# Key centring on GpSimd, fewer screening tiles on ScalarE, and six score banks, in a threshold attention kernel

## Chip, cores and metric

The kernel runs on one core of one Trainium2 chip. The metric is the device time of one execution in microseconds (us), the median of several runs. Engines are PE (TensorE, with PEld for its weight loads), DVE (VectorE), ACT (ScalarE), POOL (GpSimd) and SP (SyncE, which only issues transfers here). To evict a tile is to copy it out of PSUM, where this kernel's matmuls put their results, into SBUF, where they find their operands. The span runs from the first to the last instruction of the profiled run. The granted clock is the share of TensorE's full clock that the profile shows it was given; half-clock time is the time for which its records stand at 0.5.

## The reference

Attention over 8 x 12 heads, 512 positions, 64 dimensions, in which only weights above a threshold are kept and then normalised again:

```python
scores = einsum('bhqd,bhkd->bhqk', Q, K) / sqrt(64)
weights = softmax(scores)
weights = where(weights > 0.1, weights, 0)
weights = weights / (sum(weights) + 1e-10)
out = einsum('bhqk,bhkd->bhqd', weights, V)
```

## The kernel before

With random inputs very few rows have any weight above 0.1. The kernel screens all rows cheaply in fp16 and computes only the suspects exactly. Heads go in pairs (hp, 48 of them), and two pairs make a group q (24 groups). For each pair PE transposes keys and queries, ACT evicts the keys and sums them, the queries are evicted by ACT or DVE, and the keys are centred: 512 k - sum(k), in fp16. Eight score tiles of 128x512 per pair follow. Each is screened either by ACT (sum of exponentials) or by DVE (maximum); the table `ACT_TILES` says which. Then comes a chain per group on small tiles: flags, ranks, indices, gather of the suspect queries, exact scores, gather of a value row, scatter to the output.

```python
def do_kev(hp):                                   # ACT
    ...
    keep(nc.scalar.activation(kt[:], sc[:], ACTF.Copy, accum_out=ksum[:]))

def do_kcentre(hp):                               # DVE: the centring
    keep(nc.vector.tensor_scalar(T["qk", hp][:, 1, :], T["kt", hp][:], CS, T.pop(("ksum", hp))[:, 0:1],
                                 op0=ALU.mult, op1=ALU.subtract))

def do_sizes(hp):                                 # DVE: "sq", absolute values, reads the centred keys
    ...
    keep(nc.vector.tensor_scalar(sq..., T["qk", hp]..., 0x7FFF, None, op0=ALU.bitwise_and))

def do_screen(g, h2):
    ...
    if (h2, qi) in ACT_TILES[tiles_of(hp // 2)]:
        keep(nc.scalar.activation(junk[:], sc[:], ACTF.Exp, scale=BETA * scale / CS, accum_out=at))
    else:
        keep(nc.vector.tensor_reduce(at, sc[:], axis=AX.X, op=ALU.max))
```

The order of instructions on every engine is fixed beforehand by a small planner in the kernel. Each step is entered with an engine, the time for which it occupies it and the time to its result, both written in by hand. The engines then run their lists strictly in that order:

```python
add(("kc", hp), ("DVE", 0.46, 0.55), [("kev", hp), ("qev", hp)], g0 - 4, lambda hp=hp: do_kcentre(hp))
add(("sq", hp), ("DVE", 0.40, 0.52), [("kc", hp)], g0 + 3, lambda hp=hp: do_sizes(hp))
...
add(("qk", g), ("PE", 0.33, 0.45), [("kc", hp)], g - 2, ...)
```

The softmax here doesn't subtract the row's maximum and nothing guards it: scores larger than these inputs give would overflow.

Of the kernel before, what the change touches and what calls it, by code (L numbers as in the profile page):

```python
# [102 lines left out]
def kernel(  # L103
# [28 lines left out]
    nc = tc.nc  # L132
# [3 lines left out]
    SO = S // P  # L136
# [5 lines left out]
    scale = 1.0 / float(D) ** 0.5  # L142
# [8 lines left out]
    keep = tc.keep_in_program_order  # L151
# [8 lines left out]
    CUT = (S - 1.0) / S * math.log(max(odds, 1e-30)) - MARGIN  # L160
    CUT_SUM = 0.995 * math.exp(max(-80.0, min(80.0, BETA * CUT)))

    CS = float(S)


    ACT_TILES = ({(0, 0), (0, 1), (0, 2), (0, 3), (1, 2)},
                 {(0, 0), (0, 1), (0, 2), (0, 3), (1, 1), (1, 3)})

    def tiles_of(q):
        return 0 if q < NQ - 2 else 1  # L170
# [72 lines left out]


    cuts = consts.tile([P, 2, 2, C2], f32)
    nc.gpsimd.memset(cuts[:], CUT_SUM)
    for which in range(2):
        for h2 in range(2):
            for qi in range(SO):
                if (h2, qi) not in ACT_TILES[which]:  # L250
                    nc.gpsimd.memset(cuts[:, which, :, h2 * SO + qi], CUT * CS / scale)


    TOP_UNIT = 2.0 ** (8 * 0.0861 + 7)
# [21 lines left out]
    vpool = ctx.enter_context(tc.tile_pool(name="v", bufs=2))  # L276
    tpool = ctx.enter_context(tc.tile_pool(name="t", bufs=5))
    ktpool = ctx.enter_context(tc.tile_pool(name="kt", bufs=14))
    SC, SM = 5, 3
    spsum = ctx.enter_context(tc.tile_pool(name="spsum", bufs=SC, space=bass.MemoryType.PSUM))  # L280
    mpsum = ctx.enter_context(tc.tile_pool(name="mpsum", bufs=SM, space=bass.MemoryType.PSUM))
    junkp = ctx.enter_context(tc.tile_pool(name="junk", bufs=2))
# [6 lines left out]
    T = {}  # L289
# [20 lines left out]
    def zero_fill(q):  # L310
        fills[q] = nc.sync.dma_start(out=Oz[q], in_=zero[:])
        for s in scatters.values():
            tc.declare_no_dep(fills[q].ins, s.ins, reason="other rows of the output")
# [8 lines left out]
    def do_ktr(hp):  # L322
        T["ktr", hp] = transpose_pair(T.pop(("k", hp)))

    def do_qtr(hp):
        T["qtr", hp] = transpose_pair(T.pop(("q", hp)))

    def do_kev(hp):
        sc = T.pop(("ktr", hp))
        kt = ktpool.tile([P, SO * P], f32)  # L330
        ksum = small.tile([P, 1], f32)
        keep(nc.scalar.activation(kt[:], sc[:], ACTF.Copy, accum_out=ksum[:]))  # L332
        T["kt", hp], T["ksum", hp] = kt, ksum
# [4 lines left out]
    def do_qev(hp, eng):  # L338
        qk = tpool.tile([P, 2, SO * P], SCREEN)
        copy(eng, qk[:, 0, :], T.pop(("qtr", hp))[:])  # L340
        T["qk", hp] = qk

    def do_kcentre(hp):
        keep(nc.vector.tensor_scalar(T["qk", hp][:, 1, :], T["kt", hp][:], CS, T.pop(("ksum", hp))[:, 0:1],  # L344
                                     op0=ALU.mult, op1=ALU.subtract))


# [16 lines left out]
    def do_screen(g, h2):  # L364
        hp, qi = divmod(g, SO)
        if ("stat", hp // 2) not in T:
            stat = small.tile([P, 2, C2], f32)
            T["stat", hp // 2] = stat
        c = h2 * SO + qi
        at = T["stat", hp // 2][:, hp % 2, c:c + 1]  # L370
        sc = T.pop(("sc", g, h2))
        if (h2, qi) in ACT_TILES[tiles_of(hp // 2)]:
            junk = junkp.tile([P, SO * P], bf16)
            keep(nc.scalar.activation(junk[:], sc[:], ACTF.Exp, scale=BETA * scale / CS, accum_out=at))  # L374
        else:
            keep(nc.vector.tensor_reduce(at, sc[:], axis=AX.X, op=ALU.max))  # L376
# [169 lines left out]
    def add(name, ways, deps, prio, fn, takes=(), gives=()):  # L546
        sched.add(name, [ways] if isinstance(ways, tuple) else ways, deps, prio, fn, takes, gives)

    for hp in range(NP):
        q, n = divmod(hp, 2)  # L550
        g0 = hp * SO
        for kind, tr, fn, d in (("k", "ktr", load_k, 0.0), ("q", "qtr", load_q, 0.1)):
            add((kind, hp), ("DMA", 1.2, 3.3), [] if hp < 5 else [(tr, hp - 5)], g0 - 20 + d,
                lambda fn=fn, hp=hp: fn(hp))
        if n == 0:
            add(("z", q), ("DMA", 1.8, 4.0), [], g0 - 7.5, lambda q=q: zero_fill(q))
        ahead = [] if hp < 4 else [("qk", g0 - 3 * SO - 1), ("sq", hp - 4)]
        add(("ktr", hp), ("PE", 0.53, 0.65), [("k", hp)] + ahead, g0 - 7, lambda hp=hp: do_ktr(hp),
            takes=[("sc", ("ktr", hp))])
        add(("qtr", hp), ("PE", 0.53, 0.65), [("q", hp)] + ahead, g0 - 6, lambda hp=hp: do_qtr(hp),  # L560
            takes=[("sc", ("qtr", hp))])
        add(("kev", hp), ("ACT", 0.60, 0.85), [("ktr", hp)], g0 - 6, lambda hp=hp: do_kev(hp),
            gives=[("sc", ("ktr", hp))])
        add(("qev", hp), [("ACT", 0.47, 0.65), ("DVE", 0.60, 0.72)], [("qtr", hp)], g0 - 5,
            lambda eng, hp=hp: do_qev(hp, eng), gives=[("sc", ("qtr", hp))])
        add(("kc", hp), ("DVE", 0.46, 0.55), [("kev", hp), ("qev", hp)], g0 - 4, lambda hp=hp: do_kcentre(hp))
        add(("sq", hp), ("DVE", 0.40, 0.52), [("kc", hp)], g0 + 3, lambda hp=hp: do_sizes(hp))
        for qi in range(SO):
            g = g0 + qi
            add(("qk", g), ("PE", 0.33, 0.45), [("kc", hp)], g - 2, lambda g=g: do_qk(g),  # L570
                takes=[("sc", ("qk", g, 0)), ("sc", ("qk", g, 1))])
            for h2 in range(2):
                way = ("ACT", 0.61, 0.85) if (h2, qi) in ACT_TILES[tiles_of(q)] else ("DVE", 0.60, 0.75)
                add(("s", g, h2), way, [("qk", g)], g, lambda g=g, h2=h2: do_screen(g, h2),
                    gives=[("sc", ("qk", g, h2))])
        if n == 0:
            continue
        x = g0 + SO - 1 + LAG
        every = [("s", g, h2) for g in range(8 * q, 8 * q + 8) for h2 in range(2)]
        first = {"flags": every, "rank": [("sq", hp - 1), ("sq", hp)]}  # L580

        def stage(name, ways, deps, fn, takes=(), gives=()):
            choice = isinstance(ways, list)
            add((name, q), ways, [(d, q) for d in deps] + first.get(name, []), x,
                (lambda eng, q=q: fn(q, eng)) if choice else (lambda q=q: fn(q)), takes=takes, gives=gives)

        stage("flags", ("DVE", 0.10, 0.25), [], do_flags)
        stage("rank", ("PE", 0.75, 0.9), ["flags"], do_rank, takes=[("sm", ("rk", q))])
        stage("key", ("DVE", 0.15, 0.3), ["rank"], do_key, gives=[("sm", ("rk", q))])
        stage("oh", ("DVE", 0.62, 0.75), ["key"], do_onehot)  # L590
        stage("idx", ("PE", 0.5, 0.65), ["oh"], do_idx, takes=[("sm", ("ix", q))])
        stage("idxev", ("DVE", 0.12, 0.25), ["idx"], do_idxev)
        stage("rows", ("DVE", 0.1, 0.25), ["idx", "idxev"], do_rows, gives=[("sm", ("ix", q))])
        late = FAR if q < NQ - 3 else NEAR
        stage("gather", ("POOL", 1.2, late), ["idxev"], do_gather)
        stage("split", ("DVE", 0.2, 0.35), ["gather", "rows"], do_split)
        stage("xtr", ("PE", 0.15, 0.35), ["split"], do_xtr, takes=[("sm", ("xp", q))])
        stage("xev", [("ACT", 0.23, 0.33), ("DVE", 0.22, 0.32)], ["xtr"], do_xev, gives=[("sm", ("xp", q))])
        stage("xqk", ("PE", 1.0, 1.15), ["xev"], do_xqk, takes=[("sc", ("xs", q))])
        stage("xexp", ("ACT", 0.61, 0.85), ["xqk"], do_xexp, gives=[("sc", ("xs", q))])  # L600
        stage("xlimit", ("DVE", 0.12, 0.25), ["xexp"], do_xlimit)
        stage("xpick", ("DVE", 0.75, 0.95), ["xlimit"], do_xpick)
        stage("xone", ("DVE", 0.22, 0.35), ["xpick"], do_xone)
        stage("xto", ("DVE", 0.1, 0.25), ["xone"], do_xto)
        stage("vgather", ("POOL", 1.2, late), ["xone"], do_vgather)
        stage("scatter", ("POOL", 1.1, 3.0), ["xto", "vgather", "z"], do_scatter)
        if q == NC1 - 1:
            add(("check", 0), ("DVE", 1.8, 1.9), [("key", q)], x + 9, lambda: do_check(0))
        if q == NQ - 1:
            add(("check", 1), ("DVE", 0.35, 0.5), [("key", q)], x + 30, lambda: do_check(1))  # L610
            add(("check", 2), ("DVE", 0.3, 0.5), [("xpick", q)], x + 31, lambda: do_check(2))
# [25 lines left out]
    with tc.If(many > 0):  # L637
        with tc.For_i(0, NP, 1) as hp:
# [8 lines left out]
            kt = ktpool.tile([P, SO * P], f32)  # L647
# [69 lines left out]
```

## Time and profile before

| | before |
|---|---|
| median of 3 runs | 256.13 us (254.54 to 257.73) |
| span of the profiled run | 252.3 us |
| DVE, ACT, PE, POOL busy | 207.7, 202.1, 208.3, 82.2 us |
| mean granted TensorE clock | 0.911 |

In a row of a group, the figures after the bar are total busy us, mean ns of one, then the idle time of that engine just before such instructions and what ended it. The prediction quotes the lines that matter. It does not show the waits for scores as rows of the view of waits, which is ordered by total (columns: engine and waiting instruction, what it waited for, us in all, times, longest us):

```profile
DVE stat L376 <- PE sc L360: 9.6, 13, 2.2
ACT junk L374 <- PE sc L360: 8.1, 17, 1.1
```

### The profile page before, as it was taken

How to read it: one execution, taken by the hardware profiler on the slowest of the kernel's cores; microseconds unless marked ns; L12 is line 12 of the kernel's file. 1: busy time of each engine (PE TensorE's matmuls, PEld its weight loads, DVE VectorE, ACT ScalarE, POOL GpSimd, SP SyncE). 2: the span in 40 equal slices, each digit the busy share in tenths (PEclk: the TensorE clock that was granted, in tenths of full speed). 3: DMA queues.
4: the chain of work that ended last, by engine and by line, in shares of the span. 5: the costliest groups of instructions: out<-in, count | busy, mean ns of one | idle time of the engine just before them, and what ended most of it. 6: DMA issues, size and time to landing. Idle time of an engine off the chain costs nothing. (4 is left out here: it accounts for less than half of the span.)

```text
span 252.3 us, 5581 instructions
## 1 busy us (share of the span) xinstructions
PE 208.3 (83%) x1683; PEld 103.3 (41%) x1683; DVE 207.7 (82%) x578; ACT 202.1 (80%) x661; POOL 82.2 (33%) x121
## 2 busy tenths in 40 slices
PE   7678896898998998999898898988889998999200
PEld 3335453454443454445344544544445533324000
DVE  1788998998859999998999899999899889667220
ACT  2799998997879999987999889989989799883100
POOL 8100113334232333243163333415333213543430
PEclk9999999998979999997999799999999689559965
DMA  5899998999975898988889445564460000000000
GB/s 116 193 246 240 245 256 232 245 238 240 251 208 126 269 269 251 282 224 232 244 284 239 110 104 124 115 150 108 107 142 11 6 0 4 8 2 4 3 5 0
DMA packets 107167, 38.67 MB, mean 153 GB/s; under 512 B 103657, under 2 KB 104028, under 8 KB 107136
## 3 DMA queue, kind: packets, MB, share of 16 engines
q1 hardware_dynamic: 104832, 37.76, 56.9%
q0 software_dynamic: 2304, 0.53, 1.5%
q8 instruction: 14, 0.23, 0.4%
q14 instruction: 17, 0.14, 0.2%
HBM read 26.74 MB, written 13.37 MB: 159 GB/s over the span
## 5 line engine op out<-in xcount | busy, mean ns | idle before, releaser
L374 ACT ACTIVATE junk<-sc 128x512 bf16<-128x512 f32 x244 | 143.9, 612 | 8.6 <-PE sc L360 8.1
L376 DVE TENSOR_REDUCE stat<-sc 128x1 f32<-128x512 f32 x140 | 94.5, 684 | 10.3 <-PE sc L360 9.6
L360 PE MATMUL sc<-qk 64*128 64x512 f16 x384 | 83.3, 401 | 10.6 <-ACT junk L374 7.3
L374 ACT ACTIVATION_READ_ACCUMULATOR junk<-sc 128x1 f32 x244 | 54.2, 222 | 0.0
L508 POOL DMA_INDIRECT out_dram<-vsel,oidx x24 | 25.4, 1059 | 63.3 <-DVE rows L431 9.4
L501 POOL DMA_INDIRECT vsel<-in_V_dram,vidx x24 | 25.1, 1046 | 55.7 <-DVE oidx L497 22.1
L360 PEld LDWEIGHTS <-qk 64*128 64x128 f16 x384 | 18.2, 94 | 53.1 <-issue 49.8
L435 POOL DMA_INDIRECT qsel<-in_Q_dram,idx x24 | 25.4, 1060 | 41.8 <-DVE idx L425 30.6
L318 PE MATMUL sc<-identity_f,k_sb 128*128 128x128 f32 x192 | 33.3, 300 | 6.4 <-ACT junk L374 3.3
L332 ACT ACTIVATE kt<-sc 128x512 f32<-128x512 f32 x48 | 29.5, 615 | 6.8 <-PE sc L318 6.5
L318 PE MATMUL sc<-identity_f,q_sb 128*128 128x128 f32 x192 | 32.3, 294 | 2.0 <-ACT kt L332 1.1
L465 PE MATMUL sc<-kt,xq 128*64 128x512 f32 x96 | 30.4, 714 | 3.2 <-ACT junk L374 1.7
L318 PEld LDWEIGHTS sc<-identity_f,k_sb 128*128 128x128 f32 x192 | 21.7, 148 | 25.0 <-ACT junk L374 9.7
L472 ACT ACTIVATE e<-sc 128x512 f32<-128x512 f32 x24 | 14.4, 601 | 17.6 <-PE sc L465 17.4
L344 DVE TENSOR_SCALAR qk<-kt,ksum 128x512 f16<-128x512 f32 x48 | 24.2, 503 | 4.5 <-ACT kt L332 4.5
L318 PEld LDWEIGHTS sc<-identity_f,q_sb 128*128 128x128 f32 x192 | 23.1, 150 | 11.2 <-ACT kt L332 4.1
L336 DVE CAST qk<-sc 128x512 f16<-128x512 f32 x29 | 19.8, 686 | 7.5 <-PE sc L318 7.4
L350 DVE TENSOR_SCALAR sq<-qk 128x1024 uint16<-128x1024 uint16 x48 | 19.8, 421 | 0.3
L419 PEld LDWEIGHTS <-oh 128*128 128x128 f16 x192 | 14.4, 165 | 10.2 <-DVE oh L408 7.4
L484 DVE SCALAR_TENSOR_TENSOR pick<-e,tv,worth 128x512 f32<-128x512 f32 x24 | 17.9, 748 | 0.2
L419 PE MATMUL sm<-row_no,oh 128*128 128x4 f16 x192 | 15.4, 202 | 2.5 <-DVE oh L408 2.1
L408 DVE TENSOR_TENSOR oh<-slot_no,keys 128x1024 f16<-128x1024 bf16 x24 | 16.5, 686 | 0.0
(69 smaller groups left out, 164.2 us busy)
## 6 DMA issues: line engine op xcount, KB each, us to landing
k_sb<-in_K_dram SPq DMA_DIRECT2D x96, 128.0 KB, 3.2
q_sb<-in_Q_dram SPq DMA_DIRECT2D x96, 128.0 KB, 3.0
out_dram<-zero SPq DMA_DIRECT2D x24, 512.0 KB, 3.9
qsel<-in_Q_dram,idx POOLq DMA_INDIRECT x24, 3.2
vsel<-in_V_dram,vidx POOLq DMA_INDIRECT x24, 3.3
out_dram<-vsel,oidx POOLq DMA_INDIRECT x24, 2.5
```

What stands on the lines that cost most here:

```text
L318: keep(nc.tensor.matmul(sc[:, r * P:(r + 1) * P], lhsT=src[:, r, :], rhs=identity_f32[:], is_transpose=True, start=True, stop=True))
L332: keep(nc.scalar.activation(kt[:], sc[:], ACTF.Copy, accum_out=ksum[:]))
L336: keep(nc.scalar.copy(dst, src) if eng == "ACT" else nc.vector.tensor_copy(dst, src))
L344: keep(nc.vector.tensor_scalar(T["qk", hp][:, 1, :], T["kt", hp][:], CS, T.pop(("ksum", hp))[:, 0:1], op0=ALU.mult, op1=ALU.subtract))
L360: keep(nc.tensor.matmul(sc[:], lhsT=qk[ps, 0, qi * P:(qi + 1) * P], rhs=qk[ps, 1, :], start=True, stop=True))
L374: keep(nc.scalar.activation(junk[:], sc[:], ACTF.Exp, scale=BETA * scale / CS, accum_out=at))
L376: keep(nc.vector.tensor_reduce(at, sc[:], axis=AX.X, op=ALU.max))
L419: keep(nc.tensor.matmul(ix[:], lhsT=oh[:, c, :], rhs=row_no[:, c, :], start=(c == 0), stop=(c == C2 - 1)))
L435: keep(nc.gpsimd.indirect_dma_start(out=qsel_bufs[q % NS][:], out_offset=None, in_=Qr, in_offset=bass.IndirectOffsetOnAxis(ap=T.pop(("idx" ...
L465: keep(nc.tensor.matmul(sc[sl, :], lhsT=xq[:, sl], rhs=T.pop(("kt", 2 * q + n))[:], start=True, stop=True))
L501: keep(nc.gpsimd.indirect_dma_start(out=vsel_bufs[q % NS][:], out_offset=None, in_=Vr, in_offset=bass.IndirectOffsetOnAxis(ap=T.pop(("vidx ...
L508: s = nc.gpsimd.indirect_dma_start(out=Or, out_offset=bass.IndirectOffsetOnAxis(ap=T.pop(("oidx", q))[:, 0:1], axis=0), in_=vsel_bufs[q % ...
```

## The change

The intent is to take 24 us of centring from a full VectorE and give it to a GpSimd that is idle two thirds of the time, then move screening tiles from ScalarE to VectorE until the two balance again, and give the scores a sixth PSUM bank (SC and SM in the diff are the banks for scores and for the small chain).

```diff
-    ACT_TILES = ({(0, 0), (0, 1), (0, 2), (0, 3), (1, 2)},
-                 {(0, 0), (0, 1), (0, 2), (0, 3), (1, 1), (1, 3)})
+    ACT_TILES = (({(0, 0), (0, 1), (0, 2), (0, 3), (1, 2)}, {(0, 0), (0, 1), (0, 2), (0, 3)}),
+                 ({(0, 0), (0, 1), (0, 2), (0, 3), (1, 1), (1, 3)}, {(0, 0), (0, 1), (0, 2), (0, 3), (1, 2)}))
...   (the memsets of the cuts go from gpsimd to vector and follow the new table)
-    SC, SM = 5, 3
+    SC, SM = 6, 2
...
-        keep(nc.vector.tensor_scalar(T["qk", hp][:, 1, :], T["kt", hp][:], CS, T.pop(("ksum", hp))[:, 0:1],
+        keep(nc.gpsimd.tensor_scalar(T["qk", hp][:, 1, :], T["kt", hp][:], CS, T.pop(("ksum", hp))[:, 0:1],
                                      op0=ALU.mult, op1=ALU.subtract))
...   (the screening and its entry in the plan index the table by pair)
-        add(("kc", hp), ("DVE", 0.46, 0.55), [("kev", hp), ("qev", hp)], g0 - 4, lambda hp=hp: do_kcentre(hp))
+        add(("kc", hp), ("POOL", 0.65, 0.85), [("kev", hp), ("qev", hp)], g0 - 4, lambda hp=hp: do_kcentre(hp))
```

More of the change, by code (lines that the diff above doesn't have):

```diff
@@ L245 @@
     cuts = consts.tile([P, 2, 2, C2], f32)
-    nc.gpsimd.memset(cuts[:], CUT_SUM)
+    nc.vector.memset(cuts[:], CUT_SUM)
     for which in range(2):
-        for h2 in range(2):
-            for qi in range(SO):
-                if (h2, qi) not in ACT_TILES[which]:
-                    nc.gpsimd.memset(cuts[:, which, :, h2 * SO + qi], CUT * CS / scale)
+        for n, h2, qi in [(n, h2, qi) for n in range(2) for h2 in range(2) for qi in range(SO)]:
+            if (h2, qi) not in ACT_TILES[which][n]:
+                nc.vector.memset(cuts[:, which, n, h2 * SO + qi:h2 * SO + qi + 1], CUT * CS / scale)
     TOP_UNIT = 2.0 ** (8 * 0.0861 + 7)
@@ L371, in do_screen @@
         sc = T.pop(("sc", g, h2))
-        if (h2, qi) in ACT_TILES[tiles_of(hp // 2)]:
+        if (h2, qi) in ACT_TILES[tiles_of(hp // 2)][hp % 2]:
             junk = junkp.tile([P, SO * P], bf16)
@@ L572 @@
             for h2 in range(2):
-                way = ("ACT", 0.61, 0.85) if (h2, qi) in ACT_TILES[tiles_of(q)] else ("DVE", 0.60, 0.75)
+                way = ("ACT", 0.61, 0.85) if (h2, qi) in ACT_TILES[tiles_of(q)][n] else ("DVE", 0.60, 0.75)
                 add(("s", g, h2), way, [("qk", g)], g, lambda g=g, h2=h2: do_screen(g, h2),
```

## The prediction

> **What bounds the kernel now.** I read the page's totals first. Three engines are about equally busy, GpSimd (POOL) is not, so the totals name no single bound.
>
> ```profile
> PE 208.3 (83%) x1683; PEld 103.3 (41%) x1683; DVE 207.7 (82%) x578; ACT 202.1 (80%) x661; POOL 82.2 (33%) x121
> ```
>
> So I cut the span into stretches of 5 us (columns: stretch, its length, then busy us and instructions of PE, PE weight load, DVE, ACT, POOL, then granted TensorE clock, DMA share, GB/s).
>
> ```profile
> 60.00:65.00 5.00, 5.00 (x39) 2.43 (x38) 3.51 (x10) 3.12 (x12) 2.04 (x2) 0.66 0.94 249
> 65.00:70.00 5.00, 4.25 (x38) 2.23 (x35) 4.96 (x16) 4.95 (x18) 1.45 (x1) 1.00 0.96 260
> 70.00:75.00 5.00, 4.55 (x24) 2.25 (x24) 2.22 (x8) 3.42 (x13) 1.62 (x2) 0.66 0.78 219
> ...
> 110.00:115.00 5.00, 4.56 (x44) 1.97 (x42) 4.96 (x17) 5.00 (x18) 3.51 (x3) 1.00 0.91 250
> ...
> 235.00:240.00 5.00, 1.83 (x9) 0.59 (x9) 1.95 (x9) 0.69 (x2) 1.34 (x2) 1.00 0.01 1
> ```
>
> There are three regimes. Between 20 and 195 us, 30 of the 35 stretches have clock 1.00; in them DVE averages 4.79 of 5 us (96%) and ACT 4.66 (93%). These two bound that regime together, because every score bank is emptied by one or the other. Where the clock falls to half, PE is full and DVE and ACT starve (2.22 and 3.42 in 70 to 75). Summing (1 - clock) x 2 x 5 us from 15 to 225 gives some 31 us at half clock, 15% of the 210 us. Last, from about 230 us no tile is left to screen and a chain of small steps and gathers for the last pairs runs to the end at 252; every engine idles there. The chain of waits only covers the last 4 us, so it says nothing about the middle.
>
> The groups give the unit costs (columns: line, engine, operation, shapes, count, busy us, mean ns, idle before).
>
> ```profile
> L374 ACT ACTIVATE junk<-sc 128x512 bf16<-128x512 f32 x244 | 143.9, 612 | 8.6 <-PE sc L360 8.1
> L376 DVE TENSOR_REDUCE stat<-sc 128x1 f32<-128x512 f32 x140 | 94.5, 684 | 10.3 <-PE sc L360 9.6
> L344 DVE TENSOR_SCALAR qk<-kt,ksum 128x512 f16<-128x512 f32 x48 | 24.2, 503 | 4.5 <-ACT kt L332 4.5
> L336 DVE CAST qk<-sc 128x512 f16<-128x512 f32 x29 | 19.8, 686 | 7.5 <-PE sc L318 7.4
> L350 DVE TENSOR_SCALAR sq<-qk 128x1024 uint16<-128x1024 uint16 x48 | 19.8, 421 | 0.3
> L484 DVE SCALAR_TENSOR_TENSOR pick<-e,tv,worth 128x512 f32<-128x512 f32 x24 | 17.9, 748 | 0.2
> L408 DVE TENSOR_TENSOR oh<-slot_no,keys 128x1024 f16<-128x1024 bf16 x24 | 16.5, 686 | 0.0
> L336 ACT CAST qk<-sc 128x512 f16<-128x512 f32 x19 | 11.7, 615 | 0.7 <-PE sc L318 0.7
> L230 POOL TENSOR_SCALAR worth<-key_i 128x512 f32<-128x512 int32 x1 | 0.6, 617 | 0.1
> ```
>
> The tiles overlap their neighbours: two reductions in a row take 1.29 us in the timeline, so one occupies DVE for 0.645 us, not 0.684; screening tiles on ACT start 0.575 us apart, including the read of the accumulator. DVE and ACT waited for scores only 9.6 and 8.1 us in the whole span.
>
> [...] the only 128x512 two-operation one-input instruction on POOL (last row above) took 617 ns, against 503 ns for the centring on DVE. [...]
>
> [...] The trace shows such a meeting (start, us, what): the centring, usually 0.48 us, took 0.69 while POOL issued a gather. [...]
>
> ```profile
> 33.42 0.99 POOL L435 DMA_INDIRECT qsel<-in_Q_dram,idx  x1 [6.60 <-DVE xq L336]
> ...
> 33.95 0.69 DVE L344 TENSOR_SCALAR qk<-kt,ksum 128x512 f16<-128x512 f32 x1
> ```
>
> [...]
>
> **The change part by part.** Counts are from comparing the instruction lists of the two builds; the schedule is computed from planned times, so one edit moves other things too.
>
> 1. Centring: 48 instructions leave DVE, -24.2 us. They cost POOL 48 x 0.62 = 30 us, my estimate from the 617 ns row; POOL goes from 82 to some 112 us of about 250, which fits.
> 2. Tiles: ACT has 220 instead of 244, DVE 164 instead of 140. DVE +24 x 0.645 = +15.5, ACT -24 x 0.575 = -13.8.
> 3. The planner moves nine query evictions from DVE to ACT: DVE -9 x 0.64 = -5.8, ACT +9 x 0.6 = +5.4. Two small 128x128 copies go the same way: -0.6 and +0.6.
> 4. Thirteen set-up memsets go to DVE while it waits for the first load; near 0 on the path, and POOL reaches the first centring about 0.4 us earlier. That one waits for the end of POOL's set-up (7.5 us before), as long as it took on DVE before, so the start stays even.
> 5. PSUM six and two: PE may be one score bank further ahead, while the small chain of the previous pairs has two banks instead of three. The chain is planned ten groups behind, and PE's waits for banks from ACT (L318, 11.5 us) are not the bound at full clock. I count -1 us.
>
> Sum: DVE 207.7 - 24.2 + 15.5 - 5.8 - 0.6 = 192.6 (-15.1); ACT 202.1 - 13.8 + 5.4 + 0.6 = 194.3 (-7.8). [...] DVE's net gain is about 10, ACT's 8. They are lockstepped by banks, so I take 8.5 for the dense part, reduce it by the 15% at half clock, where PE binds, to about 7.2, subtract 1 for the sixth bank and add back about 0.5 for centrings that sit behind a gather. The tail is unchanged. 256.1 - 7.7 is 248.4; I say 248.
>
> **The rivals.**
> - Head-of-line waiting on POOL. It runs in order; its gathers and scatters wait for DVE and for landings, and a centring behind one holds back all eight score tiles of a pair. Against: the planner allows 7 us from gather to landing where the page shows 1.06 us of issue and 3.2 us to landing, so POOL's operations are placed late, and the centring is planned two groups ahead of its first matmul. For: the profile shows idle before POOL's gathers of 42 to 63 us per kind, all waits for DVE or data. If a centring loses 0.5 us on the path in half the cases, 48 x 0.25 = 12 us eat the gain: 254 to 259 us.
> - PE becomes the bound. If DVE and ACT need less, half-clock windows weigh more[...]. More of them (each costs DVE and ACT 1 to 2.5 us) would leave 251 to 253; fewer would give 244.
> - The gain is fuller than I say: centring no longer queues behind a 96% busy DVE, PE runs ahead and the starvation of DVE and ACT goes too. Then DVE's whole -15 counts, with ACT's idle filled: 241 to 244.
>
> **Range and chances.** The first and second rivals pull up, the third down, and times vary by 1.3% by themselves: 242 to 254.5. Two per cent faster is 251.0, 3 us above my centre; I give that 0.72, within two per cent 0.23, slower 0.05, which needs the head-of-line waits in full.
>
> **What would show it.** Right: DVE busy near 195 to 198 and ACT near 194, both still above 90% in full-clock stretches; centring on POOL 0.6 to 0.7 us; sq, oh or pick some tens of ns longer in the mean; the tail from last screening to end still about 24 us. Wrong: centring much longer than 0.7 us; PE waiting for POOL's qk by tens of us; DVE and ACT both below 90% at full clock; or more half-clock time than 31 us.

## The result

The changed kernel is slower: 272.63 us median (272.31 to 272.92, 4 runs) against 255.33 us (254.05 to 257.73, 4 runs). The ratio is 1.0665, 95% interval 1.0579 to 1.0752. Ratios here are the mean time of one kernel's fast runs over that of the other's in the same rounds, so not quite the ratio of the quoted medians. Executions over 1.5% slower than the fastest of the same kernel are left out of the means. Line numbers are one lower in the changed kernel: L343 is the centring (L344 before), L349 is sq (L350), L375 and L373 the screening (L376 and L374).

The page's totals for the changed kernel:

```profile
PE 219.1 (81%) x1679; PEld 108.1 (40%) x1680; DVE 201.9 (75%) x556; ACT 195.5 (72%) x624; POOL 184.0 (68%) x163
```

Its groups, from the same page:

```profile
L373 ACT ACTIVATE junk<-sc 128x512 bf16<-128x512 f32 x220 | 130.0, 609 | 23.2 <-PE sc L359 22.3
L375 DVE TENSOR_REDUCE stat<-sc 128x1 f32<-128x512 f32 x164 | 109.5, 683 | 8.5 <-PE sc L359 8.0
L343 POOL TENSOR_SCALAR qk<-kt,ksum 128x512 f16<-128x512 f32 x48 | 99.8, 2081 | 10.1 <-ACT kt L331 7.4
L349 DVE TENSOR_SCALAR sq<-qk 128x1024 uint16<-128x1024 uint16 x48 | 22.0, 458 | 27.5 <-POOL qk L343 27.5
L483 DVE SCALAR_TENSOR_TENSOR pick<-e,tv,worth 128x512 f32<-128x512 f32 x24 | 18.6, 777 | 0.1
L407 DVE TENSOR_TENSOR oh<-slot_no,keys 128x1024 f16<-128x1024 bf16 x24 | 17.5, 731 | 0.1
```

DVE and ACT did get less to do, by 5.8 and 6.6 us (the prediction had about 10, after 5 us off, by an estimate, for instructions that run beside a centring on POOL, and 7.8). But one centring took 2081 ns where the prediction had 620, and POOL's busy time went from 82 to 184 us instead of 112. Its shortest centring took 1986 ns and its median 2014, so this is no matter of a few long ones.

Where the time went is the last column of sq: DVE stood idle 27.5 us, 17 times, until POOL had finished a centring. All rows of DVE in the view of waits now sum to 55.9 us instead of 30.9, those of ACT to 59.5 instead of 35.3. For DVE the account closes: 5.8 us less busy, 25.0 us more waiting, 0.8 us less of the rest, which is the 18.4 us by which the span grew (252.3 to 270.7). Most of the new waits lie in the dense part, from 15 to 225 us: 36.0 us for DVE and 39.2 for ACT, where it was 15.5 and 19.0.

One of these waits in order of time (start, us, engine, instruction, and in brackets the idle time before it), POOL first, then DVE:

```profile
116.81 1.03 POOL L507 DMA_INDIRECT out_dram<-vsel,oidx  x1 [3.28 <-DVE one L489]
118.15 1.02 POOL L434 DMA_INDIRECT qsel<-in_Q_dram,idx  x1 [0.30 <-ACT qk L335]
119.23 4.24 POOL L343 TENSOR_SCALAR qk<-kt,ksum 128x512 f16<-128x512 f32 x2
...
117.67 0.20 DVE L402 TENSOR_TENSOR keys<-sm,flags 128x48 bf16<-128x48 f32 x1
121.26 0.43 DVE L349 TENSOR_SCALAR sq<-qk 128x1024 uint16<-128x1024 uint16 x1 [3.39 <-POOL qk L343]
121.61 1.28 DVE L375 TENSOR_REDUCE stat<-sc 128x1 f32<-128x512 f32 x2
```

POOL was held by a scatter (L507) that waited for DVE, then issued a gather, and only then began two centrings in a row. DVE reached sq of that pair at 117.9 and could not pass it until 121.26, although reductions stood behind it. The stretches around it (columns as in the prediction) show what this does to the others:

```profile
110.00:115.00 5.00, 4.44 (x30) 2.01 (x26) 4.96 (x18) 4.91 (x18) 3.06 (x3) 1.00 0.64 190
115.00:120.00 5.00, 2.94 (x40) 1.86 (x39) 2.83 (x9) 3.70 (x12) 2.83 (x3) 0.97 1.09 332
120.00:125.00 5.00, 3.72 (x19) 2.11 (x19) 3.52 (x6) 2.11 (x7) 4.54 (x3) 0.50 0.36 74
125.00:130.00 5.00, 5.00 (x23) 2.50 (x24) 2.84 (x8) 3.60 (x13) 2.90 (x2) 0.51 0.60 133
```

DVE, ACT and PE all drop together, TensorE's clock then falls to half for ten microseconds, and when work returns PE is full and the other two starve on. In the changed kernel the mean granted clock is 0.828 instead of 0.911; summed over the clock's records, which go on some 2 us past the span, half-clock time is 95 us instead of 47. In the stretch that the prediction counted, 15 to 225 us, it is 58 instead of 31.

Meetings with POOL's instructions, like the one in the prediction, are there too. Two lines of the timeline, POOL then DVE: the pick, usually 0.75 us, took 1.06 while a centring ran. It ended at 72.74 us, before the centring did at 73.50, so it was not held for the whole of it.

```profile
71.50 2.00 POOL L343 TENSOR_SCALAR qk<-kt,ksum 128x512 f16<-128x512 f32 x1
...
71.68 1.06 DVE L483 SCALAR_TENSOR_TENSOR pick<-e,tv,worth 128x512 f32<-128x512 f32 x1
```

### The profile page after: what moved, and what is told of

It reads as the page before. It is cut to its first block, busy times and chain, and to the rows that moved or that the text cites. A ratio compares the mean times of both kernels' runs of the same rounds, so it can differ in the third digit from the quotient of the medians.

```text
span 270.7 us, 5619 instructions
## 1 busy us (share of the span) xinstructions
PE 219.1 (81%) x1679; PEld 108.1 (40%) x1680; DVE 201.9 (75%) x556; ACT 195.5 (72%) x624; POOL 184.0 (68%) x163
## 5 line engine op out<-in xcount | busy, mean ns | idle before, releaser
L373 ACT ACTIVATE junk<-sc 128x512 bf16<-128x512 f32 x220 | 130.0, 609 | 23.2 <-PE sc L359 22.3
L375 DVE TENSOR_REDUCE stat<-sc 128x1 f32<-128x512 f32 x164 | 109.5, 683 | 8.5 <-PE sc L359 8.0
L343 POOL TENSOR_SCALAR qk<-kt,ksum 128x512 f16<-128x512 f32 x48 | 99.8, 2081 | 10.1 <-ACT kt L331 7.4
L373 ACT ACTIVATION_READ_ACCUMULATOR junk<-sc 128x1 f32 x220 | 48.0, 218 | 0.0
L349 DVE TENSOR_SCALAR sq<-qk 128x1024 uint16<-128x1024 uint16 x48 | 22.0, 458 | 27.5 <-POOL qk L343 27.5
L507 POOL DMA_INDIRECT out_dram<-vsel,oidx x24 | 26.0, 1082 | 23.3 <-issue 4.5
L317 PE MATMUL sc<-identity_f,q_sb 128*128 128x128 f32 x192 | 37.0, 325 | 1.6 <-ACT kt L331 0.7
L317 PE MATMUL sc<-identity_f,k_sb 128*128 128x128 f32 x192 | 36.3, 320 | 1.5 <-ACT junk L373 1.4
L464 PE MATMUL sc<-kt,xq 128*64 128x512 f32 x96 | 32.6, 762 | 1.5 <-DVE xq L335 0.7
L317 PEld LDWEIGHTS sc<-identity_f,k_sb 128*128 128x128 f32 x192 | 24.7, 162 | 21.2 <-issue 6.4
L317 PEld LDWEIGHTS sc<-identity_f,q_sb 128*128 128x128 f32 x192 | 26.0, 166 | 13.5 <-issue 4.2
L335 ACT CAST qk<-sc 128x512 f16<-128x512 f32 x28 | 16.7, 598 | 4.5 <-PE sc L317 4.5
L418 PE MATMUL sm<-row_no,oh 128*128 128x4 f16 x192 | 15.5, 203 | 5.5 <-DVE oh L407 5.1
```

Of the source, the lines that this page charges most:

```text
L317: keep(nc.tensor.matmul(sc[:, r * P:(r + 1) * P], lhsT=src[:, r, :], rhs=identity_f32[:], is_transpose=True, start=True, stop=True))
L343: keep(nc.gpsimd.tensor_scalar(T["qk", hp][:, 1, :], T["kt", hp][:], CS, T.pop(("ksum", hp))[:, 0:1], op0=ALU.mult, op1=ALU.subtract))
L349: keep(nc.vector.tensor_scalar(sq[:].bitcast(mybir.dt.uint16), T["qk", hp][:].bitcast(mybir.dt.uint16), 0x7FFF, None, op0=ALU.bitwise_and))
L418: keep(nc.tensor.matmul(ix[:], lhsT=oh[:, c, :], rhs=row_no[:, c, :], start=(c == 0), stop=(c == C2 - 1)))
L464: keep(nc.tensor.matmul(sc[sl, :], lhsT=xq[:, sl], rhs=T.pop(("kt", 2 * q + n))[:], start=True, stop=True))
L507: s = nc.gpsimd.indirect_dma_start(out=Or, out_offset=bass.IndirectOffsetOnAxis(ap=T.pop(("oidx", q))[:, 0:1], axis=0), in_=vsel_bufs[q % ...
```

## The experiments

Twelve kernels ran in three calls, and all gave correct outputs. The first two calls landed on one chip and the third on another. On the first, the kernel before varied much: 261.76 to 267.61 us and 259.41 to 271.06, its time rising as its granted clock fell (0.913 at 259.41, 0.840 at 270.93). The medians quoted take in slow runs, the ratios do not. The changed kernel itself ran only on other chips than the first.

### What one centring costs on GpSimd

```diff
+    for _ in range(2):     # kernel before, on scratch tiles, after POOL's set-up
+        ... ten forms of a one-input 128x512 instruction on gpsimd
```

> The kernel before with ten forms of a one-input 128x512 instruction on GpSimd, twice each, on scratch tiles between its set-up and its first gather. Theory (the per-partition scalar makes the form slow): every form with a [128,1] scalar takes about 2.0 us, whatever the output type or the second operation, and every form with two immediates about 0.6 us. Rival A (fp16 output of a two-operation form is slow): the fp32 outputs take about 0.6 us with and without the scalar, the fp16 ones 2.0. Rival B[...]: at least one of the two copies of each form takes about 0.6 us and the spread between copies is wide. Rival C (subtract is slow, add is fast): subtract 2.0, add 0.6. The span grows by a few us at most, from GpSimd being late for its first gather.

The groups on POOL (L283 is the very form of the change; L284 has two immediates; L285 and L286 the same pair with fp32 output; L287 multiply and add with immediates; L288 two per-partition scalars; L289 subtract alone; L290 multiply and add with a per-partition scalar and fp16 output; L291 a two-input subtract with the sum broadcast; L292 a copy):

```profile
L283 POOL TENSOR_SCALAR pd<-psrc,slot_base 128x512 f16<-128x512 f32 x2 | 4.4, 2220 | 0.2
L288 POOL TENSOR_SCALAR pd<-psrc,pcs,slot_base 128x512 f16<-128x512 f32 x2 | 4.4, 2189 | 0.0
L285 POOL TENSOR_SCALAR pd<-psrc,slot_base 128x512 f32<-128x512 f32 x2 | 4.0, 1998 | 0.0
L284 POOL TENSOR_SCALAR pd<-psrc 128x512 f16<-128x512 f32 x2 | 3.9, 1965 | 0.2
L286 POOL TENSOR_SCALAR pd<-psrc 128x512 f32<-128x512 f32 x2 | 3.9, 1926 | 0.2
L289 POOL TENSOR_SCALAR pd<-psrc,slot_base 128x512 f16<-128x512 f32 x2 | 3.1, 1572 | 0.2
L291 POOL TENSOR_TENSOR pd<-psrc,slot_base 128x512 f16<-128x512 f32 x2 | 2.1, 1041 | 0.2
L287 POOL TENSOR_SCALAR pd<-psrc 128x512 f32<-128x512 f32 x2 | 1.4, 721 | 0.2
L290 POOL TENSOR_SCALAR pd<-psrc,slot_base 128x512 f16<-128x512 f32 x2 | 1.4, 694 | 0.2
L292 POOL CAST pd<-psrc 128x512 f16<-128x512 f32 x2 | 1.2, 611 | 0.1
```

My theory, the per-partition scalar, falls: L284 and L286 have none and take 1.9 to 2.0 us. The output type (rival A) falls too, and so does rival B: the two copies of each form differ by 0.3 us at most. Rival C holds. Every scalar form with a subtract takes 1.57 us or more, and the same arithmetic with add takes 0.69 to 0.72. The two-input subtract with the second input broadcast (L291) took 1.04 us, two thirds of the one-input subtract of the same numbers (L289). The row from which the prediction took 0.62 us was a multiply and add (of int32 numbers; L287 has the same two operations on fp32). The span of this run, 275.0 us, says nothing about the forms: the probe kept POOL busy until 39.5 us, so the first gather came 14 us late.

### Each part alone

Centring back on DVE, with the new tiles and banks:

```diff
-        keep(nc.gpsimd.tensor_scalar(T["qk", hp][:, 1, :], ...       # changed kernel
+        keep(nc.vector.tensor_scalar(T["qk", hp][:, 1, :], ...
-        add(("kc", hp), ("POOL", 0.65, 0.85), ...
+        add(("kc", hp), ("DVE", 0.46, 0.55), ...
```

> The changed kernel with the centring back on VectorE; tiles 5 and 4, banks six and two stay. Theory (the slow centring on GpSimd is the whole loss): the loss goes, but VectorE carries 24 more tiles than before, so 255 to 264 us, and half-clock time is back near the 47 us of before. Rival (the tiles or the banks cost the time): stays near 272 us.

Measured: 260.24 us median against 265.85, ratio 0.9877 (0.9672 to 1.0082). The loss is gone; half-clock time is 54 us. I had expected it slower than before, for DVE's 24 extra tiles, and it is not, on this noisy chip.

Only the centring moved:

```diff
-        keep(nc.vector.tensor_scalar(T["qk", hp][:, 1, :], ...       # kernel before
+        keep(nc.gpsimd.tensor_scalar(T["qk", hp][:, 1, :], ...
-        add(("kc", hp), ("DVE", 0.46, 0.55), ...
+        add(("kc", hp), ("POOL", 0.65, 0.85), ...
```

> The kernel before with only the centring moved to GpSimd. Theory: as slow as the full change, 268 to 280 us, with the centring near 2.0 us each. Rival (the combination costs, or the banks do): 248 to 258 us.

Measured: 298.22 us median, ratio 1.1359 (1.1217 to 1.1500), more than the theory's upper end. The top waits name the same place, longer:

```profile
DVE sq L350 <- POOL qk L344: 40.0, 31, 7.1
```

So the centring by itself seems to cost more than the whole change (1.07 to 1.08, but on other chips); the tiles and banks together would then win some of it back. Half-clock time is 125 us.

Only the banks:

```diff
-    SC, SM = 5, 3        # kernel before
+    SC, SM = 6, 2
```

> The kernel before with only the PSUM split changed to six and two. Theory (banks hardly matter): within 1% of before, 253 to 258 us. Rival (two small banks hold up the chain of the previous pairs, which holds up VectorE): 261 us or more.

Measured: 259.27 us median, ratio 0.9815 (0.9691 to 0.9940). Two small banks do not hold anything up. If anything the split gains, more than the 1% of my theory and the 1 us that I counted; on this chip I would not put a size on it.

### Is the half clock a cause?

```diff
-            keep(nc.tensor.matmul(sc[:], lhsT=qk[ps, 0, ...], rhs=qk[ps, 1, :], start=True, stop=True))
+            for _ in range(2):
+                keep(nc.tensor.matmul(sc[:], lhsT=qk[ps, 0, ...], rhs=qk[ps, 1, :], start=True, stop=True))
```

In the changed kernel:

> The changed kernel with every screening matmul issued twice into the same bank, which adds activity to TensorE and nothing to the others. Theory (the extra half-clock time of the change, 95 against 47 us, follows from TensorE waiting for the centring, and itself costs only part): half-clock time falls below 60 us and the kernel is 0 to 3% faster than the plain change (ratio to before 1.03 to 1.07). Rival (the clock does not answer to activity): half-clock time stays near 95 us and the extra 384 matmuls cost 10 us or more (ratio 1.10 or more).

In the kernel before:

> The kernel before with every screening matmul issued twice. Theory: half-clock time falls from 47 us to 30 or less, the time changes by less than 2% either way, because what the clock gives the extra matmuls take. Rival (half-clock time is what costs before its spread and TensorE has room): 2 to 4% faster. Rival (TensorE has no room): 3% slower or more.

Measured: in the changed kernel half-clock time falls from 95 to 35 us and the mean clock rises to 0.941; the median is 279.37 us, and DVE still waits 23.7 us for the centring at sq. In the kernel before it falls from 47 to 12 us (clock 0.981), all of it after 245 us; the time is 263.93 us against 267.19, and its three fast runs (261.81 to 265.19) have only one fast run of before (259.41) beside them, so that is unclear. The plain change did not run on this chip, so 279.37 cannot be set against its 272 to 274 elsewhere. The two doubled kernels can be compared with each other: three fast runs each (277.59 to 280.18 and 261.81 to 265.19), and the ratio of their means is 1.059. So with half-clock time at 35 us, below the 47 of the plain kernel before, the change still costs some 6%, where the plain pairs give 6.7 and 8.2% on other chips. The clock does answer to the added matmuls (95 to 35 and 47 to 12 us at half clock), and it is not where most of the 18 us went: half-clock time mostly followed from the waits. Whether it adds one or two per cent to them stays open.

### Duration or plan? Two by two

The centring really takes 2.0 us and the plan was made with 0.65. These are two faults, and four kernels on one chip separate them. The fast form needs no added instruction: let ACT evict the negated keys, whose sum is then negated too, so that 512 k - sum(k) becomes (-512)(-k) + (-sum(k)).

```diff
-    keep(nc.scalar.activation(kt[:], sc[:], ACTF.Copy, accum_out=ksum[:]))           # changed kernel
+    keep(nc.scalar.activation(kt[:], sc[:], ACTF.Copy, scale=-1.0, accum_out=ksum[:]))
-    keep(nc.gpsimd.tensor_scalar(..., CS, ..., op0=ALU.mult, op1=ALU.subtract))
+    keep(nc.gpsimd.tensor_scalar(..., -CS, ..., op0=ALU.mult, op1=ALU.add))
-    keep(nc.scalar.activation(e[:], ..., ACTF.Exp, scale=scale, accum_out=sum1[:]))   # the exact pass
+    keep(nc.scalar.activation(e[:], ..., ACTF.Exp, scale=-scale, accum_out=sum1[:]))
```

The true plan is one number pair:

```diff
-        add(("kc", hp), ("POOL", 0.65, 0.85), ...
+        add(("kc", hp), ("POOL", 2.03, 2.15), ...
```

Both were first run on the noisy chip:

> The changed kernel with only the planner's duration of the centring on GpSimd set to what was measured (2.03 us of engine, 2.15 to the result, instead of 0.65 and 0.85). Theory (a 2 us centring is too long for one in-order engine that also issues the gathers, planned or not): still at least 3% slower than before. Rival (the loss is mostly a plan made for wrong times, so that engines wait in the wrong order): within 2% of before.

> The changed kernel with the centring on GpSimd written as multiply and add: the key eviction gives the negated keys and so the negated sum, the centring multiplies by -512 and adds the sum, and the exponential of the exact pass has its scale negated; no instruction is added. Theory (the 2.0 us of multiply and subtract, where 0.6 was taken, is the only step of the prediction that failed): the centring takes about 0.7 us, half-clock time returns to 40 to 60 us, and the ratio to before is what was predicted, 0.95 to 0.98. Rival (order on GpSimd[...] costs as well): the centring is short but the ratio is 1.00 or more, with waits for the centring left.

Measured there: true plan 259.77 us and fast form 256.48 us, beside 267.19 for before; no interval. By fast runs alone it is 257.68 and 257.97, then 251.29 and 253.90, beside one of before, 259.41. My theory for the true plan (still 3% slower) was already wrong. So all four ran again together, five rounds each:

> The changed kernel as it is, to stand beside the next three on one chip (a two by two of real duration of the centring, 2.0 or 0.7 us, and planned duration, 0.65 or 2.03). Both theories: ratio to before 1.04 to 1.08.

> Real 2.0, planned 2.03 (the earlier run with more rounds). Theory (the plan puts sq and the matmuls behind a centring that is not done, and in-order engines then wait; the 2 us alone fit on GpSimd): ratio 0.97 to 1.00, VectorE waits for the centring under 10 us instead of 27. Rival (the length itself costs): 1.02 or more.

> Real 0.7, planned 0.65 (multiply and add). Theory: ratio 0.95 to 0.98, one to three per cent below the run with real 2.0 planned 2.03, because the centring is off GpSimd's queue sooner. Rival (only the mismatch mattered): equal to it within half a per cent.

> Real 0.7, planned 2.03: the mismatch in the harmless direction. Theory (being early costs nothing, being late does): within 1% of real 2.0 planned 2.03, ratio 0.96 to 0.99. Rival (any wrong plan costs): 1.02 or more.

Measured, with 254.28 us (250.95 to 265.35, 11 runs) for the kernel before:

| real centring | planned 0.65 us | planned 2.03 us |
|---|---|---|
| 2.0 us (multiply, subtract) | 273.74 us, ratio 1.0823 (1.0748 to 1.0897) | 255.02 us, ratio 0.9990 (0.9893 to 1.0087) |
| 0.7 us (multiply, add) | 251.05 us, ratio 0.9876 (0.9784 to 0.9968) | 246.11 us, ratio 0.9681 (0.9594 to 0.9769) |

In the view of groups, one centring in the changed kernel again, then in the fast form:

```profile
L343 POOL TENSOR_SCALAR qk<-kt,ksum 128x512 f16<-128x512 f32 x48 | 100.1, 2088 | 12.4 <-ACT kt L331 8.5 <-issue 2.3
L343 POOL TENSOR_SCALAR qk<-kt,ksum 128x512 f16<-128x512 f32 x48 | 38.2, 797 | 19.2 <-ACT kt L331 13.9 <-issue 3.7
```

The waits at sq in the view of waits, in the order changed kernel again, true plan, fast form, both:

```profile
DVE sq L349 <- POOL qk L343: 27.4, 15, 6.6
```

```profile
DVE sq L349 <- POOL qk L343: 10.4, 5, 6.6
```

```profile
DVE sq L349 <- POOL qk L343: 11.2, 6, 5.3
```

```profile
DVE sq L349 <- POOL qk L343: 5.5, 2, 5.3
```

Telling the plan the truth, with the slow instruction in place and POOL busy 188.8 us, takes away the whole loss. It does so with half-clock time still at 71 us, against 47 before, which is one more sign that the clock was not the cause. The number pair changes more than order: under the long plan the planner also moves five query evictions from DVE to ACT (15 of 48 stay on DVE, not 20). That is some 3.5 us of DVE's work, so it can't be the 19 us; DVE's waits fell by 17.9 us (56.2 to 38.3), 17.0 of them at sq. Making the instruction fast under the old plan does so too, and a little more. Both together give the best kernel, 3.2% faster than before, although its plan is now wrong by 1.3 us. So a plan that errs on the late side is harmless here and one that errs on the early side costs 8%. Three expectations were missed. I had put the fast form under the old plan at 0.95 to 0.98, and it came to 0.988. The changed kernel came out at 1.082, just above 1.04 to 1.08. I had also expected the two runs with the long plan to lie within 1% of each other; they differ by 3%, so the length of the centring costs as well, when order no longer does. Why the long plan beats the fitting one by 2% for the fast form is not shown by an experiment. In the two profiled runs sq waits 5.7 us less, and ACT's rows of waits sum to 33.3 instead of 38.6 us, which is in line with centrings simply having more slack: their median is 0.70 us, but their mean 0.80 and 0.84 and their longest 1.5 and 1.7 us, and each may also sit behind a gather. A rival is the five evictions: DVE is 2.5 us less busy (199.7 to 197.2), ACT 1.3 us more. No run separates the two.

## Why the prediction was wrong

**The bound held as far as the runs show.** DVE and ACT set the pace: the best kernel's span is 8.8 us shorter than before (on another chip), with less work on both (197.2 and 194.8 us busy, before 207.7 and 202.1) and about the same waits (32.8 and 33.3 us, before 30.9 and 35.3).

**The failed step** is in part 1: "They cost POOL 48 x 0.62 = 30 us, my estimate from the 617 ns row". The term was 99.8 us, 48 x 2.08. The row was of the same engine, shape and number of operations, but its input was int32 and its second operation an add; the probe shows that the subtract is the difference (1.57 us or more, against 0.69 to 0.72 with add), not the scalar or the output type.

**The error then went through the plan.** The prediction's first rival had the mechanism, centrings behind gathers on a POOL that runs in order (above, two centrings at 119.23 us behind a scatter that had waited 3.28), and argued it down because the planner placed POOL's gathers late and the centring two groups ahead of its first matmul. That reasoning checked the planned times of the gathers and not the planned time of the centring, which the kernel had as 0.65 and 0.85 us, as short as the prediction's own 0.62. It also looked for the damage on PE ("PE waiting for POOL's qk by tens of us"): PE waited 6.3 us in its largest such row, while DVE waited 27.5, at a sq that used to follow the centring in DVE's own queue and could not be early. The rival was sized at 254 to 259 us for 0.5 us lost in half the cases; 17 waits with 27.5 us in all, up to 6.6 each, came instead. "Fits" in POOL's budget was true and beside the point: POOL at 75% busy is as fast as before under the true plan.

**Terms that held.** The end of the kernel was to stay: from the last screening on ACT (244.6 us) to the end (270.7) it is 26 us, before 24. The work moved as counted: 220 and 164 tiles, nine evictions from DVE to ACT.

**A term that held by luck.** The loss of DVE's instructions beside a centring was put at 5 us. That was my estimate: sq, oh, pick and qb are 120 instructions, centrings of 0.62 us would fill 30 of 210 us, so 17 meetings, and each was taken to cost half of 0.62, or 0.31 us; no trace had shown the half. In the changed kernel the four grew by 2.2, 1.0, 0.7 and 0.8 us, 4.7 in all (flags, not on the list, by 0.8). But the estimate was for centrings of 0.62 us. Put the measured 99.8 us and 2.08 us into the same sum and it gives 57 meetings of 1.04 us, 59 us. Counted in the trace, instruction by instruction, 55 of the 120 overlapped a centring, and only 16 of them took over 60 ns more than usual; ten of these, as the profile draws GpSimd's spans, began and ended while one and the same centring ran, like the pick above. So a meeting cost 0.09 us in the mean and not half of a centring. The 76 reductions that overlapped a centring took 683 ns, as without one. With the 0.7 us centring the same four grew by 4.2 us.

**A term that was too hopeful even so.** With the centring at the duration assumed and the plan as given, the ratio is 0.988, where 248 us against 256.1 would have been 0.968. The prediction charged 0.5 us for centrings behind gathers; DVE waited 11.2 us for them in that run. It had also overstated what leaves DVE: it took the overlap with neighbours out of the tiles (0.645 and not 0.684 us) and not out of the centring. If each instruction counts only from the end of the one before it, the 48 centrings held DVE for 20.3 us and not 24.2. Only with the long plan does the ratio come out at 0.968. That it equals the forecast is partly luck: a gain from the plan that the prediction did not contain stands in for one it had overrated. The 1 us for the sixth bank may have been too little.

**The clock.** More than 31 us at half clock was named as a sign of error, and it came: 58 us in the same stretch. The experiments make it mostly a follower of the waits. In the kernel before with every screening matmul issued twice, 47 us at half clock become 12.

## What to carry to other kernels

Before an operation moves to another engine, measure that exact form there, with its operations, scalars and types; a row of the same shape is not enough (617 ns in that row, 2081 for the centring). Where instruction order comes from a plan with typed-in durations, a moved step needs its measured duration in the plan, and a duration that is too long was the safer error here (ratio 0.968, against 1.082 for one that is too short). Then look at who reads the result on an engine that runs its list in order: here the wait appeared at sq, the consumer that used to sit behind the producer in the same queue (27.5 us).
